# High and low halves of q and k side by side in one tile, and k stacked by four transfers of 256 KB a pair

## The chip, the cores and the metric

The kernel runs on one core of one Trainium2 chip. The metric is the device time of one execution in microseconds. Before the change its median over 3 runs is 1028.84 us (1028.59 to 1028.88).

## The reference

The program is a two-layer encoder over 512 tokens of width 1024, in float32. Layer 1 mixes tokens by stick-breaking attention, layer 2 by a gated linear recurrence; each layer ends in an MLP with squared ReLU, 1024 to 4096 and back. The change touches the attention alone, which is, for each of 16 heads of width 64 and each block of 128 queries:

```python
z = einsum('bhqd,bhkd->bhqk', qb, kb) * scale
log_keep = where(mask, log_sigmoid(-z), 0)
after = cumsum(log_keep, reverse=True) - log_keep
w = where(mask, exp(log_sigmoid(z) + after), 0)
out = einsum('bhqk,bhkd->bhqd', w, vb)
```

The mask keeps keys before the query. A query block sees the keys up to its own end: 128, 256, 384 or 512 of them.

## The kernel before, in words

Everything is kept transposed: features on the 128 partitions, the 512 tokens along the row. A float32 product is made from halves: a number is split into a high half (a cast to a shorter format) and a low half (number minus high half), and products of halves are added up in one bank of the accumulator memory PSUM. For a weight slab, 128 output features of 1024 inputs, that is three products per 128 inputs (function `three`): high by high, low by high, high by low.

For the **scores** two products do. A head has only 64 features, so the high half of q fills partitions 0 to 63 of a tile and the low half partitions 64 to 127. This tile `q`, one per head, is the stationary operand. It is multiplied once with `kh`, which holds the high half of k in both partition halves, and once with `kl`, which holds the low half in both. The sum is all four products of halves.

The heads go in 8 pairs. One product of a weight slab gives q of a pair in one PSUM bank (head j in partition half j), another gives k. ScalarE casts the bank to the high half (`A.copy`, 128x512), VectorE subtracts (128x512) for the low half. Since the engines work within their partitions, the halves reach the other partition half by DMA, all issued on SyncE's queue: `stacked` sends 4 transfers of 64x512 (128 KB) for q, and 8 for k, since k's halves are each written twice. For pair 0 `first_halves` does it, with the tiles `th` and `tl` for k; for pairs 1 to 7 the halves lie in `xh` and `xl`, one buffer each, which q and k of all pairs use in turn. The k of pairs 1 to 7 is scaled first by the inverse norm (`ks`, line 373). The stacked tiles have two buffers per tag.

`score_steps` (lines 580 to 613) takes a pair: for both heads and four query blocks, two matmuls into one of two PSUM banks `z` (lines 587, 588), then ScalarE makes `w` and `keep`, two sigmoids, from the bank (595, 596), GpSimd masks the diagonal (600), VectorE runs the scan (606), GpSimd multiplies (610). For pair 0 alone VectorE multiplies the bank by the inverse norm first (`keep`, 593), and the sigmoids read that. `value_steps` transposes the weights on TensorE (628), splits them (643, 644) and multiplies by v (654, 655).

**Order.** TensorE's order is written out by hand: a list `fill` of weight products (q, k and v of the next pairs, then the output projection) is walked step by step, and score and value steps of the pairs are put between them at due times that the constants set (`SCORE0`, `PACE` and so on). Every other engine's order, SyncE's queue too, comes from the scheduler, which plans against a timeline of its own; each engine and queue then works strictly in that order. A weight slab (`slab`, lines 216 to 230) is a fetch of 512 KB into one of three buffers `raw`, two casts on ScalarE (`wh`, 227) and two subtractions on VectorE (`wl`, 229), each 128x512. The three slabs that are fetched first use line 201 for the fetch and 206 and 209 for the halves.

At the attention's end `late_slab` puts halves of three slabs of the output projection into buffers of the stacked tiles as they come free.

Of the kernel before, what the change touches and what calls it, by code (L numbers as in the profile page):

```python
# [11 lines left out]
F32 = mybir.dt.float32  # L12
# [6 lines left out]
P = 128  # L19
S = 512  # L20
# [44 lines left out]
def hybrid_encoder(  # L65
# [239 lines left out]
    with ExitStack() as actx:  # L305
# [26 lines left out]
        q, kh, kl, v, w = {}, {}, {}, {}, {}  # L332
        norm = {}

        def stacked(tag, parts):

            both = []
            for j in range(2):
                t = hp.tile([P, S], F32R, tag=f"{tag}{j}", name=f"{tag}{j}")
                for a, part in zip(half, parts):  # L340
                    nc.sync.dma_start(out=f(t[a, :]), in_=f(part[half[j], :]))
                both.append(t)
            return both

        def parted(x, tag):

            xh = hp.tile([P, S], F32R, tag=f"{tag}h", name=f"{tag}h", bufs=1)
            xl = hp.tile([P, S], F32R, tag=f"{tag}l", name=f"{tag}l", bufs=1)
            A.copy(xh, x)
            V.tensor_tensor(xl, x, f(xh), ALU.subtract)  # L350
            return xh, xl

        def q_halves(pair, ps):
            q[pair] = stacked("q", parted(ps, "x"))

        def first_halves(pq, pk):

            qh, ql = parted(pq, "x")
            h = hp.tile([P, S], F32R, tag="th", name="th", bufs=3)
            l = hp.tile([P, S], F32R, tag="tl", name="tl", bufs=3)  # L360
            A.copy(h, pk)
            V.tensor_tensor(l, pk, f(h), ALU.subtract)
            q[0], kh[0], kl[0] = [], [], []
            for j in range(2):
                for tag, two, to in (("q", (qh, ql), q), ("kh", (h, h), kh), ("kl", (l, l), kl)):
                    t = hp.tile([P, S], F32R, tag=f"{tag}{j}", name=f"{tag}{j}")
                    for a, part in zip(half, two):
                        nc.sync.dma_start(out=f(t[a, :]), in_=f(part[half[j], :]))
                    to[0].append(t)

        def k_halves(pair, ps):
            ks = hp.tile([P, S], F32, tag="ks", name="ks", bufs=1)
            V.tensor_tensor(ks, ps, norm["r"], ALU.mult)
            h, l = parted(ks, "x")
            kh[pair] = stacked("kh", (h, h))
            kl[pair] = stacked("kl", (l, l))
# [1466 lines left out]
```

## Time and profile before

| | |
|---|---|
| median of 3 runs | 1028.84 us |
| the profiled execution | 1029.37 us |
| its span, first to last instruction | 1027.5 us |
| granted TensorE clock, mean | 0.999 |
| attention, with first products | about 5 to 227 us |

In the prediction, a row of busy times by stretch reads: from:to, its length, then busy us (and instructions) of TensorE, its weight loads, VectorE, ScalarE and GpSimd, then the granted clock, the DMA engines' mean busy share and GB/s. A row of the timeline reads: start in us, us, engine, line and operation, result<-operands, size, count; in brackets the engine's idle time just before and what ended it. A row of one line's or tile's instructions reads: line, engine, operation, operands, count, then min/median/max ns and the first and last start in us. The row that begins "DMA to landing" is min/median/max us from an issue to its landing for the transfers of that answer. A row of waits reads: who waited <- for whom: us in total, times, longest. TensorE's matmuls overlap: the next starts while the last still drains.

### The profile page before, as it was taken

Reading aid. Unit: us, or ns where it says so; the run is one execution under the profiler, and the core shown is the slowest. Engines: PE = TensorE matmul, PEld = TensorE weight load, DVE = VectorE, ACT = ScalarE, POOL = GpSimd, SP = SyncE. Lnnn points to the kernel's source line nnn. Section 1 sums busy time; section 2 is a strip of 40 time slices with the busy share of each in tenths; the row PEclk is TensorE's granted clock in tenths of the full one; section 3 lists DMA queues with packets and bytes.
Section 4 is the critical chain, followed back from the end, with each engine's and each line's share of the span. In section 5 each row is a group of like instructions: output and inputs, shape, how many; then the busy total and the mean of one; then the engine's idle time right before and its main releaser. Section 6 shows DMA issues by size and latency. Waiting matters only on the chain.

```text
span 1027.5 us, 15928 instructions
## 1 busy us (share of the span) xinstructions
PE 1019.4 (99%) x5890; PEld 892.0 (87%) x5890; DVE 857.0 (83%) x1149; ACT 700.8 (68%) x1084; POOL 171.1 (17%) x237
## 2 busy tenths in 40 slices
PE   9999999999999999999999999999999999999997
PEld 7888888888888988988988888888888988988986
DVE  7988787848789898898899888984689898898898
ACT  7777676836766773873875799964755774874866
POOL 0454344420010010010011121200010110010012
PEclk9999999999999999999999999999999999999999
DMA  7745354527537667667682575452436677667653
GB/s 235 222 121 146 120 149 102 160 95 291 136 77 197 170 154 197 172 145 201 176 209 80 152 184 157 103 205 90 97 81 185 166 162 191 166 157 195 170 116 115
DMA packets 53116, 160.46 MB, mean 156 GB/s; under 512 B 6704, under 2 KB 7984, under 8 KB 53040
## 3 DMA queue, kind: packets, MB, share of 16 engines
q1 hardware_dynamic: 41952, 120.21, 35.8%
q0 software_dynamic: 10656, 38.80, 22.9%
q8 instruction: 46, 0.75, 0.3%
q10 hardware_dynamic: 432, 0.44, 0.1%
q14 instruction: 30, 0.25, 0.1%
HBM read 137.41 MB, written 4.19 MB: 138 GB/s over the span
## 4 chain that ended last, share of the span: by engine, by line
PE 90%; DVE 4%; ACT 4%; issue 1%; DMA 1%; SPq 0%; POOL 0%; DVEq 0%; ACTq 0%; POOLq 0%
PE ps_t L1135 15%; PE ps_acc L1000 9%; PE ps_acc L1135 8%; PE ps_z L1000 6%; PE ps_acc L236 5%; PE ps_acc L235 5%; PE ps_acc L234 5%; PE ps_z L1135 4%; PE ps_o L1000 3%; PE ps_t L234 2%; PE ps_t L235 2%; PE ps_t L236 2%; PE ps_o L234 2%; PE ps_o L235 2%; PE ps_o L236 2%; PE ps_z L236 2%
## 5 line engine op out<-in xcount | busy, mean ns | idle before, releaser
L789 ACT CAST wh<-b 128x1024 fp32r<-128x1024 f32 x168 | 174.0, 1051 | 116.9 <-DVE b L789 71.8
L789 DVE TENSOR_TENSOR wl<-b,wh 128x1024 fp32r<-128x1024 f32 x168 | 203.1, 1220 | 37.8 <-ACT wh L789 36.6
L1076 POOL DMA_DIRECT2D b<-in_w_dn x40 | 34.9, 874 | 364.6 <-DVE b L789 268.4
L234 PE MATMUL ps_acc<-xgh,wh 128*128 128x512 f32 x192 | 78.6, 409 | 0.0
L236 PE MATMUL ps_acc<-xgl,wh 128*128 128x512 f32 x192 | 75.3, 392 | 0.0
L235 PE MATMUL ps_acc<-xgh,wl 128*128 128x512 f32 x192 | 75.2, 392 | 0.0
L229 DVE TENSOR_TENSOR wl<-raw,wh 128x512 fp32r<-128x512 f32 (+2 forms) x70 | 62.0, 913 | 15.4 <-ACT wh L227 15.3
L789 ACT ACTIVATE u<-u 128x512 f32<-128x512 f32 x100 | 63.2, 633 | 14.2 <-DVE u L789 12.6
L606 DVE TENSOR_TENSOR_SCAN scan<-keep,later 128x128 f32<-128x128 f32 (+1 forms) x64 | 58.4, 915 | 16.7 <-ACT keep L596 10.4
L227 ACT CAST wh<-raw 128x512 fp32r<-128x512 f32 (+2 forms) x70 | 50.7, 759 | 21.1 <-PE ps_acc L236 7.3
L610 POOL TENSOR_TENSOR w<-w,scan 128x128 f32<-128x128 f32 (+1 forms) x64 | 52.8, 826 | 56.0 <-DVE scan L606 51.3
L789 DVE TENSOR_TENSOR b<-b,b 128x1024 f32<-128x1024 f32 x48 | 58.7, 1223 | 1.2
L1076 POOL DMA_DIRECT2D b<-in_w_up x24 | 20.8, 868 | 231.0 <-DVE b L789 81.1
L789 DVE TENSOR_TENSOR u<-u 128x512 f32<-128x512 f32 (+1 forms) x92 | 54.9, 597 | 4.5 <-ACT u L789 2.5
L789 ACT CAST wh<-raw 128x1024 fp32r<-128x1024 f32 x46 | 48.1, 1048 | 2.5 <-PE ps_acc L1135 2.4
L1135 PE MATMUL ps_t<-wh,bh 128*128 128x512 f32 x120 | 47.0, 392 | 0.1
L1135 PE MATMUL ps_t<-wh,bl 128*128 128x512 f32 x120 | 46.9, 391 | 0.0
L789 DVE TENSOR_TENSOR sl<-u,sh 128x512 fp32r<-128x512 f32 (+2 forms) x50 | 37.5, 750 | 10.3 <-ACT sh L789 10.3
L1000 PE MATMUL ps_z<-xgh,wh 128*128 128x256 f32 x192 | 45.0, 278 | 0.2
L789 DVE TENSOR_TENSOR wl<-raw,wh 128x1024 fp32r<-128x1024 f32 x36 | 44.3, 1231 | 0.8 <-ACT wh L789 0.8
L1000 PE MATMUL ps_acc<-low,wh 128*128 128x256 f32 x192 | 44.7, 277 | 0.0
L789 DVE TENSOR_TENSOR bl<-u,bh 128x1024 fp32r<-128x1024 f32 (+2 forms) x26 | 33.9, 1304 | 12.4 <-ACT bh L789 12.3
(418 smaller groups left out, 3218.1 us busy)
## 6 DMA issues: line engine op xcount, KB each, us to landing
b<-in_w_dn SPq DMA_DIRECT2D x48, 512.0 KB, 4.5
b<-in_w_dn POOLq DMA_DIRECT2D x40, 512.0 KB, 5.8
b<-in_w_up SPq DMA_DIRECT2D x36, 512.0 KB, 4.8
b<-in_w_up POOLq DMA_DIRECT2D x24, 512.0 KB, 5.5
raw<-in_w_m SPq DMA_DIRECT2D x16, 512.0 KB, 4.0
raw<-in_w_dn SPq DMA_DIRECT2D x16, 512.0 KB, 4.6
raw<-in_w_in SPq DMA_DIRECT2D x16, 512.0 KB, 4.0
raw<-in_w_qk SPq DMA_DIRECT2D x12, 512.0 KB, 3.7
```

What stands on the lines that cost most here:

```text
L227: A.copy(wh[:, k, :], raw[:, k, :])
L229: V.tensor_tensor(wl[:, k, :], raw[:, k, :], f(wh[:, k, :]), ALU.subtract)
L234: PE.matmul(ps, wh, ah, start=start, stop=False)
L235: PE.matmul(ps, wl, ah, start=False, stop=False)
L236: PE.matmul(ps, wh, al, start=False, stop=stop)
L606: V.tensor_tensor_scan(sc[:, S - n : S][:, ::-1], keep[:, :n][:, ::-1], later[:, S - n :][:, ::-1], 1.0, ALU.mult, ALU.max,)
L610: G.tensor_tensor(wt, wt, sc[:, S - n + 1 : S + 1], ALU.mult)
L789: ins = getattr(self.e, name)(*args, **kwargs)
L1000: PE.matmul(ps[:, i * HS : (i + 1) * HS], m, y, start=new and i == k == low == 0 and y is h, stop=(low, i, k) == steps[-1], skip_group_che ...
L1076: G.dma_start(out=unit[b].rearrange("p j n -> p (j n)"), in_=unit["src"](to), accum_op=ALU.add)
L1135: PE.matmul(sums[to][i], a[:, j, block, i * P : (i + 1) * P], y[:, j, :], start=new and g == j == n == 0 and a is h, stop=g == j == 1 and ...
```

## The change

High and low halves of q, and of k, lie side by side in one tile [128, 2, 512] (`parted`). The stacked k is one tile [128, 2, 512] per head, filled by two transfers of 64x1024 (256 KB), one to each partition half; so k takes 4 transfers a pair in place of 8. q keeps its 4 of 128 KB. The matmuls, casts and subtractions are the same in number and size. Pair 0's k now uses a buffer of the tag `k1` in place of `th` and `tl`. The single buffer `x` holds both halves, first of one operand, then of the next. `late_slab` takes its buffers from the new tags.

```diff
--- before.py
+++ after.py
@@ -329,51 +329,45 @@
             G.memset(sc[:, S : S + 1], 1.0)
             scans.append(sc)
 
-        q, kh, kl, v, w = {}, {}, {}, {}, {}
+        q, ks, v, w = {}, {}, {}, {}
         norm = {}
 
-        def stacked(tag, parts):
-
-            both = []
+        def parted(x, tag, bufs):
+
+            t = hp.tile([P, 2, S], F32R, tag=tag, name=tag, bufs=bufs)
+            A.copy(t[:, 0, :], x)
+            V.tensor_tensor(t[:, 1, :], x, f(t[:, 0, :]), ALU.subtract)
+            return t
+
+        def stack_q(pair, t, j):
+            q[pair, j] = hp.tile([P, S], F32R, tag=f"q{j}", name=f"q{j}")
+            for i, a in enumerate(half):
+                nc.sync.dma_start(out=f(q[pair, j][a, :]), in_=f(t[half[j], i, :]))
+
+        def stack_k(pair, t, j):
+            ks[pair, j] = hp.tile([P, 2, S], F32R, tag=f"k{j}", name=f"k{j}")
+            for a in half:
+                nc.sync.dma_start(out=f(ks[pair, j][a]), in_=f(t[half[j]]))
+
+        def q_halves(pair, ps):
+            t = parted(ps, "x", 1)
             for j in range(2):
-                t = hp.tile([P, S], F32R, tag=f"{tag}{j}", name=f"{tag}{j}")
-                for a, part in zip(half, parts):
-                    nc.sync.dma_start(out=f(t[a, :]), in_=f(part[half[j], :]))
-                both.append(t)
-            return both
-
-        def parted(x, tag):
-
-            xh = hp.tile([P, S], F32R, tag=f"{tag}h", name=f"{tag}h", bufs=1)
-            xl = hp.tile([P, S], F32R, tag=f"{tag}l", name=f"{tag}l", bufs=1)
-            A.copy(xh, x)
-            V.tensor_tensor(xl, x, f(xh), ALU.subtract)
-            return xh, xl
-
-        def q_halves(pair, ps):
-            q[pair] = stacked("q", parted(ps, "x"))
+                stack_q(pair, t, j)
 
         def first_halves(pq, pk):
 
-            qh, ql = parted(pq, "x")
-            h = hp.tile([P, S], F32R, tag="th", name="th", bufs=3)
-            l = hp.tile([P, S], F32R, tag="tl", name="tl", bufs=3)
-            A.copy(h, pk)
-            V.tensor_tensor(l, pk, f(h), ALU.subtract)
-            q[0], kh[0], kl[0] = [], [], []
+            tq = parted(pq, "x", 1)
+            tk = parted(pk, "k1", 2)
             for j in range(2):
-                for tag, two, to in (("q", (qh, ql), q), ("kh", (h, h), kh), ("kl", (l, l), kl)):
-                    t = hp.tile([P, S], F32R, tag=f"{tag}{j}", name=f"{tag}{j}")
-                    for a, part in zip(half, two):
-                        nc.sync.dma_start(out=f(t[a, :]), in_=f(part[half[j], :]))
-                    to[0].append(t)
+                stack_q(0, tq, j)
+                stack_k(0, tk, j)
 
         def k_halves(pair, ps):
-            ks = hp.tile([P, S], F32, tag="ks", name="ks", bufs=1)
-            V.tensor_tensor(ks, ps, norm["r"], ALU.mult)
-            h, l = parted(ks, "x")
-            kh[pair] = stacked("kh", (h, h))
-            kl[pair] = stacked("kl", (l, l))
+            t = hp.tile([P, S], F32, tag="ks", name="ks", bufs=1)
+            V.tensor_tensor(t, ps, norm["r"], ALU.mult)
+            t = parted(t, "x", 1)
+            for j in range(2):
+                stack_k(pair, t, j)
 
         def xg_step(ps, k, wh, wl):
             three(ps, xgh[:, k, :], xgl[:, k, :], wh[:, k, :], wl[:, k, :], k == 0, k == C - 1)
@@ -560,12 +554,16 @@
                 k = at[1] - self.k0
                 return self.tiles[k // 4][:, k % 4, :]
 
-        def late_slab(c, k0, tags):
+        def late_slab(c, k0, *tags):
 
             raw = wpool.tile([P, C, P], F32, tag="raw", name="raw", bufs=3)
             nc.sync.dma_start(out=raw[:, k0:, :], in_=w_so[c][:, k0:, :])
             n = (C - k0 + 3) // 4
-            tiles = [hp.tile([P, S], F32R, tag=t, name=t) for t in tags]
+            if n == 1:
+                t = hp.tile([P, 2, S], F32R, tag=tags[0], name=tags[0])
+                tiles = [t[:, i, :] for i in range(2)]
+            else:
+                tiles = [hp.tile([P, S], F32R, tag=t, name=t) for t in tags]
             for i in range(n):
                 a, b = k0 + 4 * i, min(k0 + 4 * i + 4, C)
                 h, l = (t[:, : (b - a) * P].rearrange("p (k f) -> p k f", f=P) for t in tiles[i::n])
@@ -582,10 +580,12 @@
                 for qb in range(NB):
                     n = (qb + 1) * P
                     nn = max(n, 2 * P)
-                    lhsT = q[pair][j][:, qb * P : n]
+                    lhsT = q[pair, j][:, qb * P : n]
                     z = bank("z")
-                    PE.matmul(z[:, :nn], lhsT, kh[pair][j][:, :nn], start=True, stop=False)
-                    PE.matmul(z[:, :nn], lhsT, kl[pair][j][:, :nn], start=False, stop=True)
+                    for i in range(2):
+                        PE.matmul(
+                            z[:, :nn], lhsT, ks[pair, j][:, i, :nn], start=i == 0, stop=i == 1
+                        )
                     keep = home_tile("keep", 4, "keep")
                     pool = home if qb == NB - 1 else hp
                     wt = pool.tile([P, n], F32, tag=f"w{qb}", name=f"w{qb}", bufs=3)
@@ -726,10 +726,10 @@
         done = 0
         for i in range(AHEAD, n_fill):
             if i == LATE - 14:
-                late_slab(4, EARLY, ("kh0", "kl0"))
-                late_slab(5, EARLY, ("kh1", "kl1"))
+                late_slab(4, EARLY, "k0")
+                late_slab(5, EARLY, "k1")
             if i == LATE - 8:
-                late_slab(6, 0, ("q0", "q1", "kh0", "kh1"))
+                late_slab(6, 0, "q0", "q1", "q0", "q1")
             if i == LATE:
                 x = [home_tile(tag, n, "x") for tag, n in HOMES[:7]]
                 for c in range(7):
```

The scheduler's order changes in three places around pair 0, besides the transfers themselves. On **SyncE's queue** (q, kh, kl, k are stacked tiles, `raw<-in_w` are weight fetches), from the last first fetches on, before:

```order
L201 DMA raw<-in_w_v 128x512 x4
L368 DMA q_349<-xh 64x512
L368 DMA q_349<-xl 64x512
L368 DMA kh_352<-th 64x512 x2
L368 DMA kl_355<-tl 64x512 x2
L368 DMA q_358<-xh 64x512
L368 DMA q_358<-xl 64x512
L368 DMA kh_361<-th 64x512 x2
L368 DMA kl_364<-tl 64x512 x2
L341 DMA q_421<-xh 64x512
L341 DMA q_421<-xl 64x512
L341 DMA q_424<-xh 64x512
```

and now:

```order
L201 DMA raw<-in_w_v 128x512 x4
L345 DMA q_347<-x 64x512 x2
L350 DMA k_350<-k_344 64x1024 x2
L345 DMA q_353<-x 64x512 x2
L350 DMA k_356<-k_344 64x1024 x2
L221 DMA raw<-in_w_qk 128x1024 x2
L345 DMA q_412<-x 64x512
L345 DMA q_415<-x 64x512
L345 DMA q_412<-x 64x512
L345 DMA q_415<-x 64x512
```

Two fetches of pair 2's weights, which stood behind q of pair 1 (a fourth transfer to q_424 ends that), now stand ahead of it, right behind the eight transfers of pair 0.

On **ScalarE**, from the last slab of the first fetches (L206) into pair 0's sigmoids, before:

```order
L349 CAST xh<-ps_t 128x512
L206 CAST wh<-raw 128x512 x2
L595 ACTIVATE w_440<-keep,rp 128x128
L596 ACTIVATE keep<-keep,rn 128x128
L595 ACTIVATE w_475<-keep,rp 128x256
L349 CAST xh<-ks 128x512
L596 ACTIVATE keep<-keep,rn 128x256
L595 ACTIVATE w_507<-keep,rp 128x384
L510 ACTIVATE v_526<-ps_acc,rc 128x4x64
L596 ACTIVATE keep<-keep,rn 128x384
L227 CAST wh<-raw 128x512 x2
```

and now:

```order
L338 CAST x<-ps_t 128x512
L206 CAST wh<-raw 128x512 x2
L227 CAST wh<-raw 128x512 x2
L595 ACTIVATE w_431<-keep,rp 128x128
L227 CAST wh<-raw 128x512
L596 ACTIVATE keep<-keep,rn 128x128
L227 CAST wh<-raw 128x512
L338 CAST x<-ks 128x512
L595 ACTIVATE w_459<-keep,rp 128x256
```

The casts of pair 2's weights (L227) moved from behind the third block's sigmoids to before and between the first block's.

On **VectorE**, at the same place, before:

```order
L593 TENSOR_TENSOR keep<-ps_z,r 128x128
L373 TENSOR_TENSOR ks<-ps_o,r 128x512
L593 TENSOR_TENSOR keep<-ps_z,r 128x256
L606 SCALAR_TENSOR_TENSOR scan_118<-keep,later 128x128
L593 TENSOR_TENSOR keep<-ps_z,r 128x384
```

and now:

```order
L593 TENSOR_TENSOR keep<-ps_z,r 128x128
L229 TENSOR_TENSOR wl<-raw,wh 128x512
L367 TENSOR_TENSOR ks<-ps_o,r 128x512
L229 TENSOR_TENSOR wl<-raw,wh 128x512
L593 TENSOR_TENSOR keep<-ps_z,r 128x256
L229 TENSOR_TENSOR wl<-raw,wh 128x512
L606 SCALAR_TENSOR_TENSOR scan_118<-keep,later 128x128
L593 TENSOR_TENSOR keep<-ps_z,r 128x384
```

Two subtractions for pair 2's weights now stand between the first and the second score's reading from PSUM, and one between the second and the third. Behind pair 1 the orders differ by single neighbours only.

## The prediction

> **What bounds the kernel now.** I read the page's busy line first, then the busy times by stretch, then what TensorE waited for.
>
> ```profile
> PE 1019.4 (99%) x5890; PEld 892.0 (87%) x5890; DVE 857.0 (83%) x1149; ACT 700.8 (68%) x1084; POOL 171.1 (17%) x237
> 0.00:25.00 25.00, 23.82 (x128) 19.66 (x129) 18.52 (x42) 17.97 (x35) 2.08 (x15) 1.00 0.74 235
> 25.00:227.00 202.00, 201.89 (x1222) 177.62 (x1221) 158.20 (x249) 139.40 (x302) 84.96 (x130) 1.00 0.50 141
> 227.00:1028.00 801.00, 793.72 (x4544) 694.76 (x4542) 680.25 (x858) 543.45 (x748) 84.03 (x92) 1.00 0.61 157
> PE ps_z L396 <- DVE dense_ones L118: 1.1, 1, 1.1
> ```
>
> The stretch 25 to 227 us is the attention, the only part that the change touches. TensorE works 201.89 of its 202.00 us at the full granted clock, and the list of its waits over the whole span has one row, at the very start. So TensorE sets the end, and the stacked tiles have never been late for it. Whatever the change frees on SyncE's queue or on the DMA engines was free already. It can move the end only by making TensorE wait, and the question is where the slack is thin.
>
> **The change part by part.** The transfers go first. One row holds those of the pairs 1 to 7, one those of pair 0.
>
> ```profile
> L341 SPq DMA_DIRECT2D kh<-xh x28: 461/587/965, 33.0 to 175.5; - x28
> L341 SPq DMA_DIRECT2D kl<-xl x28: 462/587/892, 35.8 to 178.1; - x28
> L368 SPq DMA_DIRECT2D kh<-th x4: 541/596/602, 22.0 to 26.7; - x4
> L368 SPq DMA_DIRECT2D kl<-tl x4: 547/597/824, 23.3 to 28.0; - x4
> DMA to landing us min/median/max: 2.2/2.4/6.6
> 54.00:57.00 3.00, 3.00 (x17) 2.53 (x16) 3.00 (x6) 1.42 (x3) 1.07 (x2) 1.00 0.89 206
> 38.00:41.00 3.00, 3.00 (x27) 3.00 (x27) 3.00 (x6) 2.38 (x7) 1.11 (x2) 1.00 1.05 265
> ```
>
> 64 transfers of 128 KB become 32 of 256 KB. At about 0.59 us an issue that is 32 x 0.59 = 18.9 us less on SyncE's queue, 2.4 us a pair, all of it beside TensorE's work: 0 on the path. The bytes stay. In 54 to 57 us, where only such transfers run, the DMA engines are already 0.89 busy at 206 GB/s; where they are backed up (38 to 41) they move 265. So the 1 MB of a pair's k takes 4 to 5 us either way, and a transfer of twice the size is no sooner done than two. The Trainium skill, "DMA: Bandwidth & Descriptors", section "Rules for kernel authors", says of two transfers to the two partition halves that they serialize on the same 16 engines; by that rule too the k tiles come no sooner, and the sum is the same. The section "Anatomy of one DMA" there gives a fixed cost of about 2 us to each transfer, which would promise 4 x 2 = 8 us a pair; the issues here are 0.59 us apart with 2.4 us to land, so that cost overlaps, and the trace does not bear out a sum of it.
>
> A **later start**: a k transfer now needs both halves, so it waits for VectorE's subtraction too. Pair 2 has the longest such delay:
>
> ```profile
> 52.73 2.39 SPq L341 DMA_DIRECT2D kh<-xh  x4
> 54.50 0.68 DVE L350 TENSOR_TENSOR xl<-ks,xh 128x512 fp32r<-128x512 f32 x1
> 55.21 2.82 SPq L341 DMA_DIRECT2D kl<-xl  x4
> 60.77 0.69 DVE L350 TENSOR_TENSOR xl<-ps_acc,xh 128x512 fp32r<-128x512 f32 x1 [1.19 <-DMA kl<-xl]
> 58.90 0.59 ACT L349 CAST xh<-ps_acc 128x512 fp32r<-128x512 f32 x1
> 60.79 0.48 ACT L596 ACTIVATE keep<-ps_z,rn 128x256 f32<-128x256 f32 x1
> 64.26 0.39 PE L587 MATMUL ps_z<-kh,q 128*128 128x512 f32 x1
> 70.96 0.28 PE L587 MATMUL ps_z<-kh,q 128*128 128x256 f32 x1
> ```
>
> The four k transfers would now be issued from 55.2 to 57.0 and land by 57.0 + 2.4 = 59.4, no later than before; this pair's scores begin at 70.96. The single buffer x, which held h and l apart, is now freed only when all four have landed, so ScalarE's cast of q at 58.90 may wait some 0.5 us where VectorE waited 1.19. ScalarE frees a score's bank there at 60.79 + 0.48 = 61.27, and the score that takes it over starts at 64.26, 3.0 us later. So I price it 0; without that cover it would be 0.5 us a pair, 3 us for the six pairs from 2 on.
>
> The **moved work** is where a price can arise. SyncE's eight instead of twelve transfers of pair 0, and q's four behind the fetches instead of ahead, bring the two 512 KB weight fetches for pair 2 forward, and the scheduler has put their casts on ScalarE and their subtractions on VectorE forward as well, among pair 0's first scores. The rows now:
>
> ```profile
> 20.76 0.52 SPq L368 DMA_DIRECT2D q<-xh  x1
> 27.36 1.24 SPq L368 DMA_DIRECT2D kl<-tl  x2
> 31.19 1.07 SPq L221 DMA_DIRECT2D raw<-in_w_qk  x2
> 25.52 1.30 DVE L209 TENSOR_TENSOR wl<-raw,wh 128x512 fp32r<-128x512 f32 x2 [0.72 <-ACT wh L206]
> 27.91 1.15 ACT L206 CAST wh<-raw 128x512 fp32r<-128x512 f32 x2
> 30.18 0.40 ACT L595 ACTIVATE w<-keep,rp 128x128 f32<-128x128 f32 x1 [1.12 <-DVE keep L593]
> 28.66 1.28 DVE L209 TENSOR_TENSOR wl<-raw,wh 128x512 fp32r<-128x512 f32 x2
> 30.66 0.69 DVE L373 TENSOR_TENSOR ks<-ps_o,r 128x512 f32<-128x512 f32 x1 [0.51 <-PE ps_o L236]
> 31.27 0.41 DVE L593 TENSOR_TENSOR keep<-ps_z,r 128x256 f32<-128x256 f32 x1
> 36.31 1.94 DVE L229 TENSOR_TENSOR wl<-raw,wh 128x512 fp32r<-128x512 f32 x2
> 33.78 0.39 PE L587 MATMUL ps_z<-kh,q 128*128 128x512 f32 x1
> 48.82 0.60 PE L628 MATMUL ps_t<-ident,w 128*128 128x128 f32 x4
> DMA to landing us min/median/max: 3.7/4.4/6.8
> 33.00:35.00 2.00, 2.00 (x18) 1.91 (x17) 1.94 (x4) 1.87 (x5) 1.02 (x2) 1.00 0.94 375
> ```
>
> Call T the time at which the first of these fetches lands. Before, they were issued at 31.19; now eight transfers of 0.6 us from 20.76 on end at about 25.6, and the first fetch goes out there (the second at 26.82, when the subtraction of 25.52 frees its buffer). By the landing times of the fetches issued at 31 to 33 us, T lies at 25.6 + 3.7, 4.4 or 6.8: 29.3, 30.0, or 32.4. The queue says more: 12 x 128 KB = 1.57 MB of pair 0 stands ahead. Begun at about 22.5 and moved at 206 to 265 GB/s it takes 7.6 to 5.9 us, to 28.4 to 30.1, and the fetch behind it takes 1.4 us at the 375 GB/s of 33 to 35: T = 29.8 to 31.5. I take 30.5, the middle of that, as the row of the queue is nearest to the case; 29.3 and 32.4 stay as ends.
>
> Behind that landing stand, in order: the first cast (1.15 / 2 = 0.58), its subtraction (1.28 / 2 = 0.64), ks (0.69), the second subtraction (0.64) and only then the multiply that reads the second score out of its PSUM bank (0.41): 2.96 us. TensorE needs that bank, one of two, for the fourth score, which it began at 33.78 (before, the bank was free at 31.27 + 0.41 = 31.68). With T = 30.5 it is free at 33.46: 0.3 us in hand, no wait. With T = 31.5 TensorE waits 0.7, with 32.4 1.6; with subtractions as slow as at 36.31 (0.97 each) 0.66 more, 2.3 at the worst. T early gains nothing, since TensorE did not wait there. ScalarE, held by its cast, puts the first scores' sigmoids from 30.18 to about T + 1.2 = 31.7; GpSimd waits for those, and nobody for GpSimd before the transposes at 48.82.
>
> The loss is not paid twice: the same two pairs of subtractions are gone from 36.31 to 39.66, so VectorE has caught up by the sixth score.
>
> I enter 0.3 us, between none at 30.5 and 0.7 at 31.5. **Sum**: the profiled execution took 1029.37 us (span 1027.5 and 1.87 around it), 0.53 above the median of 1028.84. 1029.37 + 0.3 for one like it; against the median 1028.84 + 0.3 = 1029.1.
>
> **The rivals.**
>
> Late fetch. T between 31.5 and 32.4: TensorE waits 0.7 to 2.0 us at the fourth score: 1029.5 to 1030.9. For it: one fetch issued behind the same two took the 6.8 us of the row. Against: that one had 1 MB of fetches ahead.
>
> Slower. The same wait for the same landing, with subtractions as slow as at 36.31: at T = 32.4 the fourth score waits 2.3 us: 1028.84 + 2.3 = 1031.1. It decides from T = 32.2 with slow subtractions, or 32.9 with quick ones. For it: VectorE is busy nearly all of the time there (19.93 of 20 us), so a hole in its work isn't absorbed.
>
> ```profile
> 34.00:54.00 20.00, 20.00 (x134) 18.19 (x133) 19.93 (x30) 16.70 (x35) 12.61 (x18) 1.00 0.70 221
> ```
>
> Against: the landing must come about 2 us later than the queue's bytes ask for.
>
> Faster. If TensorE did wait for each pair's stack without a row that shows it, by one issue of 0.59 us, 8 pairs would give 4.7 us: 1024.1. Against: the single row of its waits, and 201.89 of 202.00.
>
> The change doesn't do what it says. A transfer of 256 KB occupies the engines as two of 128 KB did, pair 0's tiles come no sooner, the fetch keeps its place behind them, and nothing at all shifts on the path: 1028.8.
>
> **How the numbers follow.** Forecast (0 to 0.7 us lost) 0.54; late fetch 0.22; slower 0.16; faster 0.04; no shift 0.04. A difference of 0.2%, 2.06 us, is about what a measurement of this kernel can tell from no change; so the first, second and last make "same", 0.80. The time is 1029.1. The range goes from 1028.0 (no loss, and the 0.5 us or so by which executions differ) to 1031.4 (the slower case and 0.3 for a reading of it); the 0.04 below and a longer wait are left out.
>
> **What would show it.** Right: TensorE's busy time in 25 to 227 stays within 0.5 us, 32 rows fewer on SyncE's queue, the casts of L227 on ScalarE at 30 to 31.5 and the first sigmoid just behind them, and the fourth score within 0.7 us of 33.8. Wrong: a wait of TensorE over 2 us at a score between 32 and 40 us, or one at a later pair's first score, where the k tile would be what is late; or a gain of over 2 us, which would mean that TensorE had waits that its rows do not show.

## The result, and the profile after

The changed kernel takes 1037.85 us (median of 6 runs, 1036.60 to 1039.74) against 1028.74 us before (6 runs, 1028.12 to 1029.42): 9.1 us slower, a ratio of 1.0089 with a 95% interval of 1.0079 to 1.0099. 1029.1 was forecast, with 1031.4 as the upper end. The profiled execution took 1039.74 us, 10.4 more than that of before (1029.37).

Busy times by stretch, as in the prediction, with the attention cut at 50 us. First the kernel before:

```profile
25.00:50.00 25.00, 25.00 (x166) 22.53 (x165) 22.06 (x35) 18.78 (x39) 10.14 (x16) 1.00 0.78 225
50.00:227.00 177.00, 176.89 (x1058) 155.09 (x1057) 136.14 (x215) 120.62 (x265) 74.82 (x114) 1.00 0.46 129
```

The same stretches of the changed kernel:

```profile
25.00:50.00 25.00, 22.17 (x142) 20.08 (x141) 18.12 (x31) 15.87 (x33) 7.73 (x14) 0.93 0.78 211
50.00:227.00 177.00, 173.23 (x1029) 150.46 (x1028) 138.41 (x213) 120.11 (x264) 79.40 (x116) 1.00 0.47 130
```

TensorE, busy but for 0.1 us before, now stands still in both stretches: 2.8 us at pair 0 and 3.7 us more than before over the later pairs. This busy time counts a matmul until it has drained (one of 256 columns is listed for 0.28 us, and the next starts 0.11 us after it), so a short wait hides behind a drain. Where the start-to-start distances of the matmuls are taken instead, less the median distance of their kind, and summed, the changed kernel loses 4.4 us more than before from 25 to 50 us and 5.9 us more from 50 to 250: together 10.3 of the 10.4 us. So there are **two losses**, and hardly anything (0.2 us) is lost after the attention.

What TensorE waited for (us in total, times, longest), in the changed kernel:

```profile
PE ps_z L586 <- DVE keep L593: 2.8, 1, 2.8
PE ps_o L655 <- DVE lastl L644: 1.6, 4, 0.7
PE ps_acc L497 <- DVE x L339: 0.8, 2, 0.6
PE ps_z L586 <- ACT keep L596: 0.8, 1, 0.8
PE ps_o L655 <- DVE tl L644: 0.3, 1, 0.3
```

The first row is pair 0's fourth score. The others are small and spread over the later pairs; none of them names a k tile or a DMA. Those stand one step further back, in what ScalarE and VectorE waited for:

```profile
ACT x L338 <- DMA k<-x: 11.4, 5, 3.4
ACT wh L227 <- DMA raw<-in_w_qk: 4.0, 2, 3.2
DVE x L339 <- ACT x L338: 14.6, 7, 3.2
```

The first row says that ScalarE stood five times, 11.4 us in all, before its cast of q into the buffer x, since k's transfers out of that buffer had not landed. These are the pairs 2 to 5 and 7. Pair 6 waited too, 1.7 us: that wait is listed under TensorE's transposes, but it ended 0.15 us after k's last landing, as the others did. VectorE, whose subtraction follows that cast, stood behind it.

**Pair 0** in the timeline, from the issue of the two fetches to the fourth score:

```profile
27.03 1.97 SPq L221 DMA_DIRECT2D raw<-in_w_qk  x2
33.66 1.14 ACT L227 CAST wh<-raw 128x512 fp32r<-128x512 f32 x2 [3.19 <-DMA raw<-in_w_qk]
34.31 0.69 DVE L229 TENSOR_TENSOR wl<-raw,wh 128x512 fp32r<-128x512 f32 x1 [2.75 <-ACT wh L227]
34.92 0.68 DVE L367 TENSOR_TENSOR ks<-ps_o,r 128x512 f32<-128x512 f32 x1
35.52 0.68 DVE L229 TENSOR_TENSOR wl<-raw,wh 128x512 fp32r<-128x512 f32 x1
36.12 0.42 DVE L593 TENSOR_TENSOR keep<-ps_z,r 128x256 f32<-128x256 f32 x1
36.59 1.22 PE L586 MATMUL ps_z<-k,q 128*128 128x512 f32 x2 [2.83 <-DVE keep L593]
```

The chain is the one that the prediction wrote down: cast, subtraction, ks, subtraction, multiply. It took 36.59 - 33.64 = 2.95 us from the landing, against 2.96 worked out. Only the landing was late: T is 33.64, where 30.5 was entered and 32.4 was the end of the range.

**A later pair** (4), from k's cast to that of q, in the changed kernel:

```profile
106.50 0.61 ACT L338 CAST x<-ks 128x512 fp32r<-128x512 f32 x1
107.23 0.78 DVE L339 TENSOR_TENSOR x<-ks,x 128x512 fp32r<-128x512 f32 x1
108.08 3.15 SPq L350 DMA_DIRECT2D k<-x  x4
114.01 0.47 ACT L596 ACTIVATE keep<-ps_z,rn 128x256 f32<-128x256 f32 x1
116.24 0.59 ACT L338 CAST x<-ps_acc 128x512 fp32r<-128x512 f32 x1 [1.76 <-DMA k<-x]
116.72 1.14 ACT L227 CAST wh<-raw 128x512 fp32r<-128x512 f32 x2
116.86 0.69 DVE L339 TENSOR_TENSOR x<-ps_acc,x 128x512 fp32r<-128x512 f32 x1 [1.59 <-ACT x L338]
```

The four transfers go out behind the subtraction, the last one lands at 116.06, and q's cast starts 9.1 us after the end of k's. Before, it started 7.3 us after it, and without a wait:

```profile
100.58 0.61 ACT L349 CAST xh<-ks 128x512 fp32r<-128x512 f32 x1
108.47 0.59 ACT L349 CAST xh<-ps_acc 128x512 fp32r<-128x512 f32 x1
```

### The profile page after: what moved, and what is told of

Its sections match the earlier page's. It is cut to its first block, busy times and chain, and to the rows that moved or that the text cites. A ratio compares the mean times of both kernels' runs of the same rounds, so it can differ in the third digit from the quotient of the medians.

```text
span 1038.0 us, 15906 instructions
## 1 busy us (share of the span) xinstructions
PE 1023.6 (99%) x5890; PEld 894.8 (86%) x5890; DVE 858.6 (83%) x1149; ACT 700.3 (67%) x1084; POOL 175.3 (17%) x237
## 4 chain that ended last, share of the span: by engine, by line
PE 85%; DMA 4%; DVE 4%; ACT 3%; issue 1%; SPq 1%; POOL 0%; ACTq 0%; DVEq 0%; POOLq 0%
PE ps_t L1135 16%; PE ps_acc L1000 9%; PE ps_acc L1135 8%; PE ps_z L1000 7%; PE ps_o L1000 4%; PE ps_z L1135 4%; PE ps_acc L234 4%; PE ps_acc L235 4%; PE ps_acc L236 4%; DMA k<-x 2%; PE ps_t L236 2%; PE ps_t L235 2%; PE ps_t L234 2%; PE ps_o L234 2%; PE ps_z L236 2%; PE ps_z L234 2%
## 5 line engine op out<-in xcount | busy, mean ns | idle before, releaser
L227 ACT CAST wh<-raw 128x512 fp32r<-128x512 f32 (+2 forms) x70 | 50.7, 758 | 23.9 <-PE ps_acc L236 7.1
L600 POOL TENSOR_SCALAR_AFFINE_SELECT w<-w 128x128 f32<-128x128 f32 x64 | 35.5, 555 | 86.0 <-ACT w L595 85.7
L789 DVE TENSOR_TENSOR sl<-u,sh 128x512 fp32r<-128x512 f32 (+2 forms) x50 | 37.5, 750 | 10.3 <-ACT sh L789 10.3
```

The source lines that it names most:

```text
L227: A.copy(wh[:, k, :], raw[:, k, :])
L600: G.affine_select(t, t, pattern=[[-1, P]], compare_op=ALU.is_gt, fill=0.0, base=0, channel_multiplier=1,)
L789: ins = getattr(self.e, name)(*args, **kwargs)
```

## The experiments

Theory A: the early fetch at pair 0, whose casts stand in front of other work. Theory B: the single buffer x, which comes free too late for q's cast. Rivals: C, the size of the transfers itself; D, the joint tile. Differences are to the kernel before as timed on the same chip in the same comparison.

| kernel | median us | to before | ratio (95%) |
|---|---|---|---|
| the change | 1037.85 | +9.1 | 1.0089 (1.0079 to 1.0099) |
| q in two buffers | 1031.61 | +2.7 | 1.0028 (1.0018 to 1.0037) |
| fetches and casts behind | 1035.09 | +6.2 | 1.0058 (1.0045 to 1.0071) |
| both | 1028.37 | -0.6 | 0.9994 (0.9985 to 1.0003) |
| q in two buffers, casts alone held | 1028.55 | -0.7 | 0.9993 (0.9985 to 1.0002) |
| the same again | 1028.75 | -0.4 | 0.9995 (0.9987 to 1.0004) |
| eight transfers of 128 KB | 1028.72 | -0.2 | 0.9997 (0.9988 to 1.0005) |
| before, low halves first | 1031.94 | +2.7 | 1.0023 (1.0013 to 1.0033) |
| fetches behind, short rows | 1035.41 | +6.1 | 1.0062 (1.0049 to 1.0076) |
| the change, halves alternating | 1036.18 | +6.9 | 1.0071 (1.0057 to 1.0085) |
| fetches behind, q's cast later | 1032.92 | +3.9 | 1.0036 (1.0022 to 1.0050) |
| the change again | 1037.66 | +8.5 | 1.0090 (1.0074 to 1.0105) |

### Two buffers for q

```diff
...
         def q_halves(pair, ps):
-            t = parted(ps, "x", 1)
+            t = [hp.tile([P, S], F32R, tag="early", name="xq") for _ in range(2)]
+            A.copy(t[0], ps)
+            V.tensor_tensor(t[1], ps, f(t[0]), ALU.subtract)
```

In the differences here, `...` stands for lines of code that are not shown. q's high and low half are now two tiles apart from x, taken from the buffers of the tag `early`.

> The change with one thing altered: q of the pairs 1 to 7 gets a high and a low tile out of the two buffers of `early`, so that ScalarE's cast of q no longer waits until all of k's transfers have landed. Order around pair 0 as in the change.
>
> The profile of the change has TensorE lose 4.4 us from 25 to 50 us and about 5.7 us in small pieces over the later pairs. Theory B (the single buffer x, released by the landing of k, delays ScalarE and VectorE, and through them TensorE, pair by pair): the row of ScalarE's waits for k's landings, 11.4 us in 5, goes, and some 5 us with it: 1032 to 1034, ratio to the kernel before 1.003 to 1.005. Theory A (all of the loss is the late fetch at pair 0 and what follows from it): no change, 1037 to 1039. Theory C (256 KB transfers are slow, and whoever reads the k tiles is late): no change either, and a wait of TensorE for a k tile appears.

Measured: 1031.61, 6.2 us less than the change and just under the expected 1032 to 1034. Busy times by stretch of this kernel:

```profile
25.00:50.00 25.00, 22.38 (x148) 19.85 (x147) 18.69 (x31) 16.21 (x33) 8.66 (x15) 1.00 0.75 208
50.00:227.00 177.00, 176.90 (x1061) 155.07 (x1060) 138.04 (x217) 121.93 (x267) 74.73 (x116) 1.00 0.47 132
```

The later pairs are whole again (176.90; before 176.89), and pair 0's loss stays. The transfers of k are still four of 256 KB and land as late as in the change; where nobody waits for the buffer, that costs nothing. Theory B holds for the later pairs, rival C falls for them.

### Fetches and casts behind, and both edits

```diff
...
+                if pair == 2:
+                    fetch_after[0] = lastq[1].ins
+                    first = keeps[2].ins
+                else:
+                    first = norm["copy"].ins
-                with tc.issue_after(norm["copy"].ins):
+                with tc.issue_after(first):
                     halves = slab(w_qk[i, pair], CUT)
...
```

`lastq` is q's last transfer of a pair, `keeps` lists the scores' second sigmoids; the fetch inside `slab` is issued behind `fetch_after`. So the fetches go behind q's transfers of pair 1, and their casts behind the third score's sigmoid, as before the change.

> The change, with pair 2's weight fetches held behind q's transfers of pair 1 on SyncE's queue, and their casts behind the third score's sigmoid on ScalarE, as in the kernel before. Four transfers of 256 KB and the single buffer x stay.
>
> Theory A (the early fetch, landed at 33.64, holds ScalarE and VectorE in front of the fourth score; then the granted clock is 0.5 for 3.4 us): the 4.4 us of 25 to 50 us are back, TensorE's wait of 2.8 us at line 586 is gone: 1033 to 1034, ratio 1.004 to 1.005. Theory B alone (all is the buffer): no change, 1037 to 1039. Rival (the wait only moves, since casts and subtractions that are put off collide with later scores): back less than 2 us, and a new wait between 36 and 50 us.

> The two edits together: q's halves in two buffers of their own, and the fetches held behind q's transfers. Four transfers of 256 KB stay.
>
> Theories A and B together make up all of the loss: 1028 to 1030, ratio 0.999 to 1.001, and the size of the transfers costs nothing where nobody waits for them. Theory C (the size itself costs): 2 us or more stay, 1031 and above, with waits for a k tile or for k's buffers in TensorE's or ScalarE's rows.

Measured: 1035.09 for the order alone, 1028.37 for both. Busy times by stretch of the order alone:

```profile
25.00:50.00 25.00, 25.00 (x167) 22.45 (x165) 22.21 (x36) 18.66 (x39) 9.10 (x16) 1.00 0.77 221
50.00:227.00 177.00, 174.05 (x1033) 151.27 (x1032) 135.76 (x211) 117.65 (x259) 79.42 (x114) 1.00 0.45 129
```

This is the mirror image: pair 0 is whole, the later pairs aren't. The two losses add up: 2.7 (what the two buffers left) and 6.2 (what the order left) make 8.9 of the 9.1 us, and with both edits nothing is left. The expectation for the order alone, 1033 to 1034, was 1 us short: it took pair 0's share from one profile of the change, in which a drop of the clock was added (below).

### The casts alone held

As both edits, but the fetches stay as early on SyncE's queue as in the change; only the casts are held.

> The change with q's halves in two buffers of their own (1031.6 us) and, beside that, the casts of pair 2's slab held behind the third score's sigmoid on ScalarE. The fetches stay ahead of q's transfers on SyncE's queue, as in the change.
>
> Theory A in its narrow form (the price at pair 0 is that casts of a slab not yet landed stand in front of the first sigmoids on ScalarE and of the second score's multiply on VectorE; the fetch itself may be early): 1028 to 1029.5, as with both edits together. Rival (the fetches ahead of q's transfers cost something themselves: q of pair 1 lands at 38 instead of 32): 1030 to 1032.

Measured: 1028.55, and 1028.75 in a second comparison. So the early fetch itself costs nothing. The price of pair 0 is the place of the fetched slab's casts in ScalarE's order and of its subtractions in VectorE's: in the change they stand ahead of the first score's sigmoid and the second score's multiply, and both engines wait there for a landing that they don't need yet. The second comparison was also to tell whether this kernel beats the one before:

> The kernel with q in two buffers and the casts held, once more: it came out at 0.9993 of the kernel before, 0.9985 to 1.0002. If the 40 SyncE instructions that it saves, or anything else in it, are worth something, 0.9985 to 0.9995 again; if it is only level with the kernel before, 0.9990 to 1.0010.

0.9993 and 0.9995, both with 1 inside the interval: level, as far as this can tell. (On SyncE it has 41 instructions fewer, 32 of them transfers, the rest semaphore instructions.) Its second profile shows that pair 0 stands close to an edge in any case: the tiles of pair 0 landed about 3 us later there than in the first (the first k tile was whole at 29.68 instead of 26.45, behind first weight fetches that landed 2.4 us later), and TensorE waited for k directly.

```profile
PE ps_z L598 <- DMA k<-k: 1.3, 1, 1.3
```

### Eight transfers of 128 KB in the change's tiles

```diff
+        def part_k(pair, t, j, i):
+            for a in half:
+                nc.sync.dma_start(out=f(ks[pair, j][a, i, :]), in_=f(t[half[j], i, :]))
...
-                stack_k(pair, t, j)
+                ks[pair, j] = hp.tile([P, 2, S], F32R, tag=f"k{j}", name=f"k{j}")
+            for i in range(2):
+                for j in range(2):
+                    part_k(pair, t, j, i)
...
```

> The change with its tiles (halves side by side, one buffer x), but k stacked by eight transfers of 128 KB in the order of the kernel before (high halves first).
>
> Theory C (the size of the transfers is the cause: in the change four of 256 KB land 1.07 us apart, 245 GB/s, where the kernel before landed eight of 128 KB in 2.63 us, about 400 GB/s, when they were backed up): transfers land 1 to 2 us sooner, the buffer x comes free in time, and nearly all is back: 1028.5 to 1031, ratio 1.000 to 1.002. Rival D (the joint tile is the cause: it is released only as a whole, and the low half of k waits for the whole of it, whatever the size of the transfers): the later pairs lose their 5 us as in the change, 1033 to 1036. The first fetch stands ahead of q's transfers of pair 1 here as in the change, so theory A alone leaves up to 4 us: 1032 to 1033.

Measured: 1028.72, all of it back. Rival D, the joint tile by itself, is out. The number is the one that theory C named, but this doesn't show that size is the cause: with the size, two other things came back. High halves start before the subtraction again, and the scheduler placed work otherwise. Nor does the ground of theory C hold: the eight small transfers did land within 2.63 us, but from 106 to 108.9 us the DMA engines moved 209 GB/s, not 400. A part of the bytes had moved before (104 to 106 us: 340 GB/s, with a weight fetch). The next run takes the size away from the other two.

### Before, with k's low halves first

```diff
...
-            kh[pair] = stacked("kh", (h, h))
             kl[pair] = stacked("kl", (l, l))
+            with tc.issue_after(sent[0].ins):
+                kh[pair] = stacked("kh", (h, h))
```

`sent` is the last transfer that `stacked` issued. The scheduler moved some weight fetches on SyncE's queue and casts on ScalarE along with it.

> The kernel before with one thing altered: for the pairs 1 to 7 the four transfers of k's low half go ahead of the four of its high half on SyncE's queue. Eight transfers of 128 KB, the tiles xh and xl apart; only, none of them starts before VectorE's subtraction, and the buffer xh, which ScalarE's cast of q needs, comes free last instead of first.
>
> Theory B in the form that two buffers gave it (what costs is when the buffer for q's cast comes free, by the start after the subtraction and the release with the last landing, and neither the size of a transfer nor the joint tile): the loss of the later pairs appears in the kernel before, up to the 6.2 us that two buffers gave back: 1032 to 1036, with ScalarE's waits for k's landings in its rows. Theory C (the size of the transfers): no change, 1028.5 to 1029.5.

Measured: 1031.94, +2.7, at the low end of what theory B expected: the kernel before, with its small transfers and its separate tiles, becomes slower by the order of its eight issues and what the scheduler moved with it. The time from the end of k's cast to the landing that frees the buffer for q, read for the pairs 2 to 7 in each trace, and when q's cast then started (means, us), beside ScalarE's waits for k's landings there:

| kernel | first issue | buffer free | q's cast | ScalarE waits | to before |
|---|---|---|---|---|---|
| before | 0.1 | 4.7 | 6.6 | 0 | |
| eight of 128 KB | 0.1 | 7.4 | 7.9 | 1.6 in 1 | -0.2 |
| before, low first | 1.5 | 8.8 | 9.2 | 5.1 in 3 | +2.7 |
| fetches behind, cast later | 1.6 | 9.1 | 9.9 | 3.9 in 3 | +3.9 |
| fetches behind | 1.6 | 8.8 | 8.9 | 10.5 in 5 | +6.2 |
| both edits | 1.5 | 9.0 | 6.6 | 0 | -0.6 |

In the row of the fetches behind, pair 6's wait of 1.7 us is again listed under TensorE and not counted.

Low halves first frees the buffer at 8.8 us with eight transfers of 128 KB, and the change's four of 256 KB, with the fetches behind, do so at 8.8 too. **For when the buffer comes free, the size sets nothing here.** What does is that no transfer starts before the subtraction (1.5 us instead of 0.1), that the buffer waits for the last landing instead of the fourth of eight, and what went ahead on the queue meanwhile. In the pairs 2, 3 and 7 a weight fetch that stood behind k's transfers now stands ahead of them, in the change and in the last four kernels of the table alike. Pair 2 before:

```profile
55.21 2.82 SPq L341 DMA_DIRECT2D kl<-xl  x4
58.07 1.30 SPq L221 DMA_DIRECT2D raw<-in_w_qk  x1
```

and in the change:

```profile
58.01 0.33 SPq L221 DMA_DIRECT2D raw<-in_w_qk  x1
59.12 3.46 SPq L350 DMA_DIRECT2D k<-x  x4
```

k's first transfer in these pairs lands 4.1, 4.4 and 3.6 us after its issue, before 2.2 us. In the pairs 4 to 6 a fetch was in flight ahead of k before the change too. ScalarE waits 1.7 to 1.8 us in those pairs of the change, and 2.4, 2.1 and 3.4 us in the pairs 2, 3 and 7. The kernel with both edits has the fetch ahead too and loses nothing, so it can cost only through the buffer; no run moves it alone, so its share isn't shown.

Pair 5 of the kernel with the low halves first, from the issues to q's cast:

```profile
128.40 2.40 SPq L341 DMA_DIRECT2D kl<-xl  x4
130.89 2.47 SPq L341 DMA_DIRECT2D kh<-xh  x4
133.29 1.16 ACT L227 CAST wh<-raw 128x512 fp32r<-128x512 f32 x2
135.21 0.59 ACT L349 CAST xh<-ps_acc 128x512 fp32r<-128x512 f32 x1 [0.76 <-DMA kh<-xh]
```

Then the change with the fetches behind:

```profile
129.56 3.00 SPq L353 DMA_DIRECT2D k<-x  x4
136.25 0.59 ACT L339 CAST x<-ps_acc 128x512 fp32r<-128x512 f32 x1 [1.69 <-DMA k<-x]
136.74 1.14 ACT L228 CAST wh<-raw 128x512 fp32r<-128x512 f32 x2
```

From first issue to last landing it is 6.7 us with the small transfers (135.11) and 6.6 with the large (136.16). But the price is 2.7 us in one and 6.2 in the other. The rows show a difference that goes with it: with the small ones the scheduler had placed the slab's casts ahead of q's, so ScalarE stood 0.76 us, with less behind it; with the large ones q's cast stands ahead of them, and ScalarE stood 1.69. It is the same in the pairs 3 to 7.

The Trainium skill, "Perfetto Trace Analysis", section "DMA Optimizations", notes that splitting transfers into smaller ones may let some start sooner. The kernel before and the change are that rule read backwards: the joined halves started 1.5 us behind k's cast instead of 0.1, with the DMA engines no more than 0.47 busy from 50 to 227 us.

### q's cast later on ScalarE

```diff
...
+        def hold_cast(pair, ps):
+            waiting.append((len(keeps), pair, ps))
...
+                if waiting and len(keeps) > waiting[0][0]:
+                    with tc.issue_after(keeps[-1].ins):
+                        q_halves(*waiting.pop()[1:])
```

The cast of q is emitted only once another score's sigmoids are out, and is ordered behind them.

> The change with the order of the kernel before around pair 0 (1035.1 us), the single buffer x and four transfers of 256 KB, and ScalarE's cast of q of the pairs 2 to 7 put behind the next score's sigmoids instead of ahead of them. The buffer comes free no sooner; only, less work stands behind the cast while it waits.
>
> Theory B in the form that the low halves first left (the price is ScalarE standing idle in its order, with sigmoids and other casts behind the waiting cast; where the scheduler had put the cast later, no wait and no loss was seen): 1028.5 to 1031. Rival (q itself is late, and whoever needs q or its PSUM bank waits, wherever the cast stands): 1034 to 1036, with TensorE's wait for the bank `ps_acc` grown.

Measured: 1032.92, between the two. ScalarE's waits for k fell from 10.5 to 3.9 us and 2.3 us came back (+6.2 to +3.9), so the place of the cast is a part of the price. The rest found another way out, which the rival had named: q's PSUM bank is held until its cast and subtraction, and TensorE now waits for that bank, 3.0 us where the kernel with the fetches behind had 1.0. (Its profile also has a wait of 0.7 us at pair 0 that the other's lacks.)

```profile
PE ps_acc L506 <- DVE x L340: 3.0, 4, 1.7
```

### Rows and halves

Two looks at the transfers. In the first, on top of the kernel with the fetches behind, x got 64 bytes between its halves (`[P, 2, S + 16]`), so that 256 KB go as 128 rows of 2048 bytes. In the second the four transfers of the change alternate between the partition halves.

> The change with the order of the kernel before around pair 0 (1035.1 us), and x with 64 bytes between its high and low half, so that a transfer of 256 KB consists of 128 rows of 2048 bytes instead of 64 of 4096.
>
> If the long rows make the transfers slow (a row of 4096 bytes takes about 0.27 us of a DMA engine, one of 2048 bytes 0.14 and, backed up, 0.105 to 0.113): landings of one pair come less than 1 us apart, the buffer is free sooner, 1031 to 1034. If what counts is the start alone: landings as far apart, 1034 to 1036.

> The change with the four transfers of k's 256 KB in another order: each goes from another partition half to another one than the one ahead of it (first to first, second to second, first to second, second to first); at pair 0 all of q goes ahead of k.
>
> If two transfers between the same halves hinder each other, four land sooner than the 7.5 us from the first issue to the last landing of the change, by 1 us or more, and 1 to 4 us come back: 1034 to 1037. If not, 1037 to 1039.

Measured: 1035.41, the same as with long rows; in pair 5 the landings lie 1.58, 1.13 and 1.14 us apart, with long rows 1.47, 1.20 and 1.05. Alternating gave 1036.18, 1.7 us less than the change and within the range that was named for quicker landings, but not by them: the buffer is free 9.0 us after k's cast (8.9 in the change), TensorE's busy time in 50 to 227 is no better, and the gain lies at pair 0, where that kernel sends all of q ahead of k, the first fetch landed at 31.53 instead of 33.64, and the scheduler put the second score's multiply ahead of one of the subtractions.

Busy times by stretch of the alternating kernel:

```profile
25.00:50.00 25.00, 24.31 (x156) 21.31 (x155) 20.41 (x34) 17.97 (x37) 10.00 (x16) 1.00 0.73 207
50.00:227.00 177.00, 173.03 (x1026) 150.07 (x1025) 136.58 (x211) 118.35 (x260) 78.06 (x114) 1.00 0.47 130
```

The Trainium skill, "DMA: Bandwidth & Descriptors", section "Rules for kernel authors", says that transfers to the two partition halves share the same engines and serialize. Four transfers one behind the other, whichever halves they join, agree with it.

### The change again

> The change itself, profiled once more. In its first profile TensorE stood still for 3.0 us at the fourth score, and the granted clock was then 0.5 for 3.4 us; with q in two buffers it stood still for 2.6 us at the same place, and the clock stayed at 1.00. If the length of the pause alone decides, the clock halves again for about 3.4 us behind a pause of about 3 us. If it is a matter of where the pause happens to lie, it may stay at 1.00 with the same pause. Time 1036 to 1039 in either case.

Measured: 1037.66, ratio 1.0090. The second profile can't decide between the two expectations, since its pause was shorter: the first fetch landed at 32.74 instead of 33.64, and TensorE waited 1.7 us. The clock stayed at 1.00. The stretch behind the pause, first in the first profile of the change, where TensorE had waited 2.8 us:

```profile
36.00:39.50 3.50, 2.91 (x11) 2.72 (x12) 3.36 (x7) 2.69 (x6) 0.64 (x2) 0.51 0.85 257
```

then in the second:

```profile
36.00:39.50 3.50, 3.50 (x30) 3.41 (x29) 3.26 (x7) 2.87 (x7) 0.82 (x2) 1.00 0.82 248
```

The second profile loses 2.7 us more than the kernel before from 25 to 50 us and 6.1 from 50 to 250, by the start-to-start distances. These are the shares that the medians of the two single edits gave; what the first profile lost beyond them at pair 0, 1.7 us, goes with the halved clock and the later landing.

## Why the prediction was wrong

**What bounds the kernel: right, with a wrong inference.** TensorE does set the end, and it never waits for a k tile. But "the stacked tiles have never been late for it" was read as if only the tiles could be late. The losses came over ScalarE and VectorE, whose orders hold other work behind a wait for a DMA.

**Transfers: right.** 32 issues fewer on SyncE's queue are worth nothing by themselves: with the waits removed, the kernel is level with the one before (0.9993 to 0.9995). The large transfers are no sooner done: 6.6 us from the first issue to the last landing of pair 5's k, against 6.7 with small ones. The fixed cost of about 2 us, which the prediction quotes and declines to add up, is given by the Trainium skill, "DMA: Bandwidth & Descriptors", section "Anatomy of one DMA — SWDGE (gpsimd) path", for transfers issued from GpSimd. Those of k are issued on SyncE; in pair 5 they land 1.05 to 1.47 us apart, so no such sum is paid.

**Later start: wrong, and the larger share.** This step priced the wait for the buffer x at 0 and, without cover, at 0.5 us a pair, 3 us in all. Measured: 6.2 us, about 1 us for each of the six pairs from 2 on. It had the mechanism, the buffer that is freed only when all four have landed, and failed twice in the size. The landing: "issued from 55.2 to 57.0 and land by 57.0 + 2.4" took 2.4 us from small transfers 0.6 us apart that found the engines free. The paragraph above it had said that 1 MB takes 4 to 5 us, and before the change VectorE's subtraction at 60.77 had already waited for a landing of kl, at 60.65. Nor did the step look at what goes ahead on the queue: one of the single neighbours by which the orders were said to differ behind pair 1 is the weight fetch that passes all of k's transfers. In the kernel with the fetches behind, whose pair 2 is issued at about the forecast time (55.04), that fetch lands at 57.56, the first transfer of k at 59.14 and the last one at 62.52 instead of 59.4, and q's cast waits 2.9 us instead of 0.5. The cover: it was looked for in one PSUM bank that ScalarE frees, 3.0 us early. The price was paid elsewhere, by the work that stands behind the cast on two engines (the subtractions `lastl` and `tl` that the value products need) and by q's own bank `ps_acc`. Naming what is queued behind the waiting instruction on each engine would have shown both.

**Moved work: the chain right, T wrong.** The wait is T + 2.96 - 33.78. With the T of the first profile of the change, 33.64, that is 2.82, and 2.83 was measured; in the change again and with q in two buffers it gives 1.9 and 2.1, and 1.7 and 2.5 were measured. T was put at 30.5 (29.3 to 32.4); five profiles in which both fetches go out early have 32.5 to 33.6, and a sixth, the alternating kernel, 31.5. Three terms of it failed. The first fetch went out at 27.03, not at 25.6. The stack of pair 0 was done at 30.72, not by 28.4 to 30.1; it was taken to begin at 22.5, but the last of the first fetches landed only at 25.07 (before the change, 24.05). And the fetch behind it took 2.9 us, not the 1.4 that 375 GB/s gave: two fetches and then q's transfers were in flight at once, 1 MB of fetches landed in 35.86 - 30.72 = 5.1 us, 204 GB/s. "Not paid twice" was right: pair 0 costs 2.7 us in the medians, and nothing of it is left after 50 us in the kernel with two buffers.

**The rivals.** "Late fetch" and "slower" (0.22 and 0.16) name what happened at pair 0, a wait at the fourth score for a late landing, but neither has its size. T was 33.64 where they end at 32.4, and the subtractions, which "slower" took as slow, were quick, 0.60 us from start to start; that its wait of 2.3 us comes near the measured 2.8 is luck. Against "slower" it was held that "the landing must come about 2 us later than the queue's bytes ask for", though the fetch had been priced at 375 GB/s, the highest rate among the prediction's rows. No rival had the loss of the later pairs. "No shift" and "faster" are out.

**What would show it.** Two of the signs named for a wrong forecast came true or nearly so: a wait of TensorE over 2 us at a score between 32 and 40 us, and one at the later pairs, though through a bank and `lastl` rather than a k tile.

Open is how the price of the later start splits between the late start, the weight fetch that went ahead in three pairs, and the scheduler's placing of the casts: low halves first cost 2.7 us with the buffer free as late as in the change and the same fetches ahead, and there the scheduler had put the casts in another order. Putting the cast later in the change brought 2.3 us of the 6.2, not all.

## What to carry to other kernels

Joining two transfers into one makes the joint transfer wait for the later of its sources and frees the source only with the last byte: follow the single buffer to its next writer, then everything that is queued behind that writer on its engine, and what the scheduler lets pass ahead of the transfer while it can't start. A price for a moved fetch is the place of its consumers in the in-order engines, more than its place on the queue: holding the casts alone gave pair 0's loss back. And when a transfer meets a busy queue, price its landing by the bytes ahead of it at the slow end of the rates in the trace, not by the landing time of transfers that met a free one.

## What the runs showed of the hardware

After TensorE's pause of 2.8 us in the first profile of the change the granted clock was 0.5 for 3.4 us (36.06 to 39.47; it fell 2.3 us into the pause), and a matmul of 256 columns took 0.41 us instead of 0.28. After pauses of 2.5 us (q in two buffers) and 1.7 us (the change again) at the same place it stayed at 1.00:

```profile
36.00:39.50 3.50, 3.50 (x29) 3.41 (x30) 3.16 (x6) 3.44 (x9) 0.92 (x2) 1.00 0.78 258
```

The Trainium skill, "TensorE: Matmul & The Clock Gate", section "Part 1: The HAM clock gate (the "warmup" mystery)", has half clock after an idle window of about 3.4 us that runs freely. The 3.4 us of half clock agree with the window; the pause that brought it was shorter than one. In each trace the moments at which the granted clock changes lie whole multiples of 3.413 us apart: in the first profile of the change 30.72 us, nine of them, from 5.34 to 36.06. Counted on in that step, the window that ended with the fall held 2.3 us of the pause, which began at 33.76. With q in two buffers a boundary at 34.89 parts the pause (33.43 to 35.88) into 1.5 and 1.0 us, and in the change again all of the 1.7 us lie in one window. So the idle share of one window fits the three cases, and the pause's length does too; three pauses can't tell which decides.

A row of 4096 bytes costs the DMA engines here what two of 2048 bytes do: among pair 5's transfers of k the median is 0.295 us of an engine with long rows and 0.149 with short ones, and with either, four transfers of 256 KB between partition halves land 1.05 to 1.58 us apart.
